# An earlier load gate, reordered matmuls and a different last product in a fused matmul, Gelu, matmul kernel

## Chip, cores and metric

One Trainium2 chip, one of its cores. The metric is the device time of one execution in microseconds. All runs quoted are of the fast state. The profile's span is about 1.75 us shorter than the measured time of the same execution (120.5 against 122.23 before, 119.0 against 120.74 after). Times inside an execution are counted from the span's start.

## The reference

```python
m, k, n, p = 1024, 1024, 2048, 1024          # a: m x k, b: k x n, c: n x p, all float32
h = np.matmul(a, b)
h = 0.5 * h * (1 + np.tanh(np.sqrt(2 / np.pi) * (h + 0.044715 * h ** 3)))
return np.matmul(h, c).astype(np.float32)
```

## The kernel before

Half of the first product (1024 of the 2048 columns of b) is computed directly, transposed (hT = b^T a^T), in bf16. The other half of it, and all of the second product, run as a seven-product scheme of the Strassen kind ("Seven"): sums of operands are made on VectorE, seven products of half the size on TensorE, and the results are added up. The two products of operands as they are (P1, P2) are bf16; the five with a sum in them are f32r, a float32 form that the traces call fp32r. A product's result is added up in a bank of PSUM, from which ScalarE or VectorE takes it.

Loads come on two queues. SP's queue brings the f32 data that must be there first: pieces of a (512 KB, `load_a(h, q)`), to be cast and transposed, and half-pieces of b (`load_b(q, c)`). GpSimd's queue casts to bf16 on the way: the other pieces of a, the slices k=4..7 of b, then the rest of b and c. A one-element copy, `gate`, holds this queue back until a given f32 load has landed.

```python
load_a(0, 0); load_b(0, 0); load_a(1, 0); load_a(0, 1)      # f32 loads one to four
load_b(1, 0); load_a(1, 1); load_b(0, 1); load_b(1, 1)      # five to eight

nc.gpsimd.tensor_copy(gate, sta[:, 1, 1, 3, 0:1])           # waits for load six
...                                                         # then GpSimd issues a, b[k=4..7], b2, c

block(0, range(4), (0, 1))              # bf16 matmuls of slices k=0, 1
turn1(1, 0, 5, cast_a(1, 0, nc.vector))  # cast, 8 transposes on TensorE, copy out
turn1(0, 1, 7, cast_a(0, 1, nc.scalar))
...
block(1, range(3), (0, 1))
cast_b(2, 0); cast_b(3, 0)              # ScalarE
ab = cast_a(1, 1, nc.vector)            # load six
block(0, range(4), (2,))
turn1(1, 1, 7, ab)
block(0, range(4), (3,))
for k in range(KH):                     # KH = 4, KT = 8
    cast_b(k, 1)                        # ScalarE: loads seven and eight
for t in range(4):
    leave(0, t)                         # empties PSUM banks, ScalarE for even t
...
for h, t in T2[:7]:                     # seven tiles, k=0..3 done before
    mm1(ps[h, t], t, h, range(KH, KT))  # k=4..7, tile by tile
    gelu(t, h, ps[h, t])
```

The second product, `two`, by stages (X are PSUM banks 0 to 3, Y banks 4 to 7):

```python
for j in range(4):                                   # P1: A11 B11, bf16
    w.product(px[j], A11, B11, j, True)
    p1[j] = snap("m", px[j], "p1")                   # ScalarE keeps a copy
for j in range(4):                                   # P2: A12 B21, bf16
    p = bank(Y[j])
    w.product(p, A12, B21, j, True)
    done(0, 0, j, plus(p, p1[j]))                    # VectorE add, store of C11
...                                                  # P5, P6, P7, P3: f32r
for j in range(4):                                   # P4, last: C21, VectorE copy, store
    w.product(px[j], w.s[3], w.last_t, j, False)
    done(1, 0, j, px[j])
```

## Time and profile before

| | before |
|---|---|
| time, median of 4 | 122.32 us (122.23 to 122.36) |
| profiled span | 120.5 us |
| TensorE (PE) busy | 112.4 us, 93% |
| VectorE (DVE) busy | 88.4 us, 73% |
| last matmul ends | 116.72 us |
| from there to the end of the span | 3.75 us |

TensorE is the bound, but a busy share of 93% does not say where the missing time is. Three questions do: where between two matmuls is there a hole (the timeline and the wait view of PE), what ended it, and what comes after the last matmul. The prediction shows these lines.

### The profile page before, as it was taken

To read this page: it belongs to the slowest core of one execution; us is meant where nothing else is said; L and a number is where in the kernel's file an instruction comes from. 1 tells how busy PE (TensorE), PEld (TensorE's weight loads), DVE (VectorE), ACT (ScalarE), POOL (GpSimd) and SP (SyncE) were. 2 spreads that over 40 slices of the span, in tenths; PEclk is the share of its full clock that TensorE was granted. 3 is DMA by queue.
4 is the path that set the end of the run, shared out by engine and by line. 5 is a ranking of instruction groups with operands and counts; after the bars stand their busy time and mean duration, and the time that the engine had idled before them with its cause. 6 is when DMAs were issued, how large, how long until landed. Compare 5 with 4: busy or idle time off the path is not lost.

```text
span 120.5 us, 1459 instructions
## 1 busy us (share of the span) xinstructions
PE 112.4 (93%) x550; PEld 72.7 (60%) x550; DVE 88.4 (73%) x92; ACT 53.3 (44%) x86; POOL 14.6 (12%) x27
## 2 busy tenths in 40 slices
PE   6985999969999999999999999999999999999970
PEld 2633545624444444888888444468888888888850
DVE  0243589488017899978779999979999996892490
ACT  4046490005637779946669636900012595100000
POOL 2000895462322000000000000000000000000000
PEclk9999999999999999999999999999999999999997
DMA  2999999999999999997000000062000002004695
GB/s 85 283 371 367 305 167 202 168 205 207 207 207 213 212 212 209 212 212 145 1 5 0 5 0 0 0 250 98 0 0 0 5 0 87 0 0 174 235 352 197
DMA packets 11463, 16.86 MB, mean 140 GB/s; under 512 B 705, under 2 KB 5825, under 8 KB 11457
## 3 DMA queue, kind: packets, MB, share of 16 engines
q0 software_dynamic: 5952, 8.39, 40.1%
q1 hardware_dynamic: 5504, 8.39, 19.8%
q8 instruction: 4, 0.07, 0.2%
q14 instruction: 3, 0.02, 0.1%
HBM read 20.97 MB, written 4.19 MB: 209 GB/s over the span
## 4 chain that ended last, share of the span: by engine, by line
PE 62%; DMA 21%; DVE 6%; POOL 4%; SPq 2%; issue 1%; ACT 1%; DVEq 0%; ACTq 0%
PE ps L239 50%; PE ps L112 12%; DMA b<-in_b_dram 8%; DMA sta<-in_a_dram 8%; DMA out_dram<-ot 5%; DVE x L197 4%; POOL a L93 2%; DVE ot L285 2%; POOL b L96 1%; SPq L68 1%; SPq L71 1%; DVE ot L370 1%; ACT u L280 1%; POOL gate L82 0%; DVEq L285 0%
## 5 line engine op out<-in xcount | busy, mean ns | idle before, releaser
L112 PE MATMUL ps<-aT,b 128*128 128x512 bf16 x128 | 29.2, 379 | 1.7 <-DMA b<-in_b_dram 1.2
L239 PE MATMUL ps<-x,s 128*128 128x512 f32 x128 | 29.6, 391 | 0.0
L239 PEld LDWEIGHTS ps<-x,s 128*128 128x128 f32 x128 | 24.0, 188 | 5.1
L112 PEld LDWEIGHTS <-b 128*128 128x128 bf16 x128 | 12.1, 98 | 15.9 <-DMA b<-in_b_dram 2.0
L239 PE MATMUL ps<-x,x 128*128 128x512 f32 x64 | 14.8, 389 | 0.0
L239 PE MATMUL ps<-c_sb,hT 128*128 128x512 bf16 x64 | 14.0, 379 | 0.0
L239 PEld LDWEIGHTS ps<-x,x 128*128 128x128 f32 x64 | 12.0, 188 | 2.5
L280 ACT ACTIVATE v<-ps 128x512 f32<-128x512 f32 x8 | 4.8, 599 | 17.1 <-PE ps L239 17.1
L116 ACT ACTIVATE hT<-ps 128x512 bf16<-128x512 f32 x12 | 6.8, 595 | 12.1 <-PE ps L112 12.1
L239 PE MATMUL ps<-x 128*128 128x512 f32 x48 | 11.3, 393 | 0.0
L239 PEld LDWEIGHTS <-hT 128*128 128x128 bf16 x64 | 6.2, 97 | 7.6 <-issue 0.3
L270 DVE TENSOR_TENSOR half<-ps,half 128x512 f32<-128x512 f32 x8 | 5.5, 692 | 7.0 <-PE ps L112 6.6
L239 PEld LDWEIGHTS ps<-x 128*128 128x128 f32 x48 | 9.0, 188 | 2.0
L197 DVE TENSOR_TENSOR x<-c_sb 128x1024 fp32r<-128x1024 bf16 x8 | 9.2, 1215 | 0.0
L285 DVE TENSOR_TENSOR ot<-ps,v 128x512 f32<-128x512 f32 x8 | 5.3, 687 | 4.6 <-DMA out_dram<-ot 3.8
L141 ACT ACTIVATE b<-stb 128x512 bf16<-128x512 f32 (+1 forms) x9 | 4.7, 573 | 6.6 <-DMA stb<-in_b_dram 6.6
L285 DVE TENSOR_TENSOR ot<-ps,u 128x512 f32<-128x512 f32 x8 | 5.4, 691 | 3.0 <-ACT u L280 3.0
L116 ACT ACTIVATE hT<-ot 128x512 bf16<-128x512 f32 x12 | 7.0, 624 | 1.2 <-DVE ot L285 1.2
L239 PE MATMUL ps<-aT,b 128*128 128x512 bf16 x32 | 7.1, 379 | 0.0
L102 POOL DMA_DIRECT2D c_sb<-in_c_dram x8 | 5.7, 712 | 8.9 <-DMA b<-in_b_dram 8.9
L280 ACT ACTIVATE p<-ps 128x512 f32<-128x512 f32 x8 | 4.6, 594 | 4.8 <-PE ps L239 4.8
L116 ACT ACTIVATE hT<-half 128x512 bf16<-128x512 f32 x8 | 5.0, 631 | 2.6 <-DVE half L270 2.6
(47 smaller groups left out, 114.7 us busy)
## 6 DMA issues: line engine op xcount, KB each, us to landing
c_sb<-in_c_dram POOLq DMA_DIRECT2D x8, 512.0 KB, 20.2
out_dram<-ot SPq DMA_DIRECT2D x16, 256.0 KB, 2.1
sta<-in_a_dram SPq DMA_DIRECT2D x4, 512.0 KB, 6.9
stb<-in_b_dram SPq DMA_DIRECT2D x4, 512.0 KB, 8.9
b<-in_b_dram POOLq DMA_DIRECT2D x4, 512.0 KB, 13.8
a<-in_a_dram POOLq DMA_DIRECT2D x4, 256.0 KB, 5.6
b<-in_b_dram POOLq DMA_DIRECT2D x4, 256.0 KB, 8.9
```

The source lines that it names most:

```text
L68: nc.sync.dma_start(out=sta[:, h, q], in_=av[:, 4 * h:4 * h + 4, ds(q * 256, 256)])
L71: nc.sync.dma_start(out=stb[:, c, 2 * q:2 * q + 2], in_=bv[:, 2 * q:2 * q + 2, ts(c, H)])
L93: nc.gpsimd.dma_start(out=st, in_=av[:, 4 * h + m:4 * h + m + 2, ds(KH * 128, H)])
L102: nc.gpsimd.dma_start(out=c_sb[:, t:t + 2], in_=cv[:, t:t + 2])
L112: nc.tensor.matmul(p, b1[:, k, ts(t, 128)], aT[:, h, k], start=(k == k0), stop=(k == k1 - 1))
L116: nc.scalar.activation(hT[h][:, t], p, AF.Gelu_apprx_tanh)
L141: nc.scalar.activation(b1[:, k, ds(c * H + i * (H // n), H // n)], stb[:, c, k, r], AF.Copy)
L197: nc.vector.tensor_tensor(out=dst[:, r], in0=x[:, r], in1=y[:, r], op=op)
L239: nc.tensor.matmul(p[:, ds(c0, w)], l[:, k, ts(j, 128)], r[:, k, ds(c0, w)], start=(start and k == 0), stop=(k == self.kt - 1), skip_group ...
L270: nc.vector.tensor_tensor(out=half[:, h, t], in0=p, in1=half[:, h, t], op=ADD)
L280: nc.scalar.activation(st, p, AF.Copy)
L285: nc.vector.tensor_tensor(out=ot, in0=p, in1=st, op=ADD)
```

## The change

It has four parts. The gate looks at load five instead of load six. Three matmuls are put in front of the transposes that waited for ScalarE. In the first product the slices k=4..7 go over four tiles slice by slice. And in the second product the C11 tile j=3 keeps its P1 in a buffer of its own in SBUF until the end, while its P2 product (eight matmuls of 512 columns) becomes the last work of the kernel, in two column halves of 256, each added and stored by itself.

The diff leaves out the hunks that only fold the function `last` into `done`.

```diff
-    nc.gpsimd.tensor_copy(gate, sta[:, 1, 1, 3, 0:1])
+    nc.gpsimd.tensor_copy(gate, stb[:, 0, 3, 0:1])
@@
-    turn1(0, 1, 7, cast_a(0, 1, nc.scalar))
     for t in range(3):
         ps[1, t] = bank(4 + t)
-    block(1, range(3), (0, 1))
+    ab = cast_a(0, 1, nc.scalar)
+    block(1, range(3), (0,))
+    turn1(0, 1, 7, ab)
+    block(1, range(3), (1,))
@@
-    for h, t in T2[:7]:
-        mm1(ps[h, t], t, h, range(KH, KT))
+    for k in range(KH, KT):
+        for h, t in T2[:4]:
+            mm1(ps[h, t], t, h, (k,))
+    for n, (h, t) in enumerate(T2[:7]):
+        if n >= 4:
+            mm1(ps[h, t], t, h, range(KH, KT))
         gelu(t, h, ps[h, t])
@@ (P1)
-            p1[j] = snap("m", px[j], "p1")
+            if w is two and j == 3:
+                p1[j] = pieces("ab", 2, [128, H], F32, "p1")
+                nc.scalar.activation(p1[j], px[j], AF.Copy)
+            else:
+                p1[j] = snap("m", px[j], "p1")
@@ (P2)
-        for j in range(4):
+        for j in range(4 if w is one else 3):
@@ (after P4)
+        if w is two:
+            for i in range(2):
+                r = ds(i * 256, 256)
+                p = bank(Y[i])
+                w.product(p, A12, B21, 3, True, i * 256, 256)
+                ot = pieces("e", 2, [128, 256], F32, "ot")
+                nc.vector.tensor_tensor(out=ot, in0=p[:, r], in1=p1[3][:, r], op=ADD)
+                store(3, i * 256, 256, ot)
```

More of the change, by code (lines that the diff above doesn't have):

```diff
@@ L323, in seven @@
             w.product(px[j], w.s[3], w.last_t, j, False)
-            if w is one or j < 3:
-                done(1, 0, j, px[j])
-            else:
-                last(px[j])
+            done(1, 0, j, px[j])
+        if w is two:
[6 more added lines that the diff above has]
+                store(3, i * 256, 256, ot)
     one.s1()
@@ L372, in done2 @@
         store(4 * i + j, l * H, H, p)
-    def last(p):
-        done2(1, 0, 3, p)
     def between2(n):
```

## The prediction

> **What bounds the kernel now.** I read the page first. Its chain of waits is almost all TensorE from 27 us on, and before that it is loads:
>
> ```profile
> span 120.5 us, 1459 instructions
> ...
> PE   6985999969999999999999999999999999999970
> ...
> PE ps L239 50%; PE ps L112 12%; DMA b<-in_b_dram 8%; DMA sta<-in_a_dram 8%; DMA out_dram<-ot 5%; DVE x L197 4%; POOL a L93 2%; DVE ot L285 2%; POOL b L96 1%; SPq L68 1%; SPq L71 1%; DVE ot L370 1%; ACT u L280 1%; POOL gate L82 0%; DVEq L285 0%
> ```
>
> The first line with PE is its busy tenths in 40 slices, the second the chain by line. The row of tenths shows where time is still to be had: slices 2 to 4 (3 to 12 us), the "6" of slice 9 (24 to 27 us), and the tail. Everything between 27.3 and 116.7 us is dense, so a change pays there only by taking out TensorE work. TensorE's waits and its timeline name the holes:
>
> ```profile
> PE pt L135 <- ACT ab L106: 1.3, 1, 1.3
> ...
> PE ps L112 <- DMA b<-in_b_dram: 1.2, 2, 0.8
> ...
> 10.93 0.62 PE L135 MATMUL pt<-ident,ab 128*128 128x128 bf16 x8 [1.31 <-ACT ab L106]
> ...
> 13.55 0.61 PE L135 MATMUL pt<-ident,ab 128*128 128x128 bf16 x8
> ...
> 24.30 1.46 PE L112 MATMUL ps<-aT,b 128*128 128x512 bf16 x6
> ...
> 26.09 0.39 PE L112 MATMUL ps<-aT,b 128*128 128x512 bf16 x1 [0.34 <-DMA b<-in_b_dram]
> 27.33 1.04 PE L112 MATMUL ps<-aT,b 128*128 128x512 bf16 x4 [0.85 <-DMA b<-in_b_dram]
> ```
>
> The first product has four banks ready at 25.2 us, but it goes tile by tile: after two matmuls of its first tile (k=4, 5) it waits for slice k=6 (26.09) and k=7 (27.33). Counted by starts at 0.216 us each, 26.09-25.59 plus 27.33-26.31 is 1.5 us lost (the wait view says 1.2, as it counts a matmul as busy until its modelled end).
>
> The loads before that run on two queues. The f32 queue (SP) brings eight 0.52 MB loads; the casting queue (POOL) starts when the gate copy sees load six:
>
> ```profile
> 11.13 1.15 ACT L141 ACTIVATE b<-stb 128x512 bf16<-128x512 f32 x2 [0.25 <-DMA stb<-in_b_dram]
> ...
> 12.64 0.18 POOL L82 COPY gate<-sta 128x1 f32<-128x1 f32 x1 [11.33 <-DMA sta<-in_a_dram]
> 12.68 0.69 DVE L108 CAST ab<-sta 128x1024 bf16<-128x1024 f32 x1 [0.40 <-DMA sta<-in_a_dram]
> ...
> 13.96 1.15 ACT L141 ACTIVATE b<-stb 128x512 bf16<-128x512 f32 x2 [1.68 <-DMA stb<-in_b_dram]
> ...
> 15.27 1.15 ACT L141 ACTIVATE b<-stb 128x512 bf16<-128x512 f32 x2 [0.15 <-DMA stb<-in_b_dram]
> ...
> 16.32 2.04 ACT L106 ACTIVATE half<-ps 128x512 f32<-128x512 f32 x4
> ```
>
> So loads 5, 6, 7 and 8 land at about 11.1, 12.6, 13.95 and 15.25. The tail:
>
> ```profile
> 109.30 7.42 PE L239 MATMUL ps<-x,s 128*128 128x512 f32 x32
> ...
> 114.62 2.03 DVE L370 COPY ot<-ps 128x512 f32<-128x512 f32 x3
> 116.83 0.69 DVE L370 COPY ot<-ps 128x512 f32<-128x512 f32 x1 [0.18 <-PE ps L239]
> ```
>
> The last matmul ends at 116.72; copy 0.69, store about 2.1 (the page's time to landing of a store), close 0.8 us. The chain in order of time also reaches 116.8 by a second way, vector add, store, vector add, each waiting for an output buffer; it ends in the same 0.1 us as TensorE, so both must move for the end to move.
>
> **What the Trainium skill says.** "TensorE: Matmul & The Clock Gate", "Wait — 56ns, not 53.3ns?": warm back-to-back matmuls start N/2.4 GHz plus about 2.5 ns apart, 215.7 ns at 512 columns and 55.6 at 128. The trace agrees: 59 matmuls in 12.90 us from 28.63, so (12.90-0.38)/58 = 0.216 us, and eight transposes in 0.61 give 0.056. By the same formula 256 columns cost 0.109 (an estimate; this trace has none). "DMA: Bandwidth & Descriptors", "Queues, rings and completion order": each engine takes turns between the queues it has work for, packet by packet. So a casting load started sooner takes bandwidth from the f32 loads still under way; before shows hardly any such overlap. Same page, "Anatomy of one DMA — SWDGE (gpsimd) path": a DMA has a fixed cost of about 2.0 us plus bytes over 436 GB/s. For stores here the trace has 2.1 us for 256 KB, so the fixed part must be smaller, about 1.4.
>
> **The change part by part.**
>
> 1. Slice by slice. Sixteen matmuls (k=4..7 on four banks) replace the tile-by-tile order. Slice k is first used at 25.16, 26.03, 26.89, 27.75; k=6 and k=7 were there at 26.05 and 27.3 even before. No wait is left: -1.5 us, with no matmul added. The Gelus come in a bunch of four (0.60 each), but banks 0 to 3 are wanted again only after 20 more matmuls (4.3 us), so they hide.
>
> 2. The first reordering. Three matmuls that wait only for the copy ending 10.35 go ahead of the transposes that waited for ScalarE until 10.93. TensorE fills 10.4 to 11.05, but the next thing, the transposes at 13.55, needs the VectorE cast 12.68+0.69 = 13.37 of load six, which nothing moves. So of 0.6 us filled only about 0.12 us survives (13.55 to 13.43).
>
> 3. The gate looks at load five, not six: casting starts 1.5 us sooner (11.13 for 12.64). Gain alone: with part 1, the b slices are no longer what TensorE waits for, so **nothing**. Cost: loads seven and eight now share the engines. Summing half-microsecond windows of DMA, 3.70 MB of the f32 queue's 4.19 have moved by 13.0 us; that is about when casting data should begin (gate 11.2 plus the 1.4 to 1.9 us seen between the gate at 12.64 and the drop of the rate at 14.0 to 14.5). The remaining 0.5 MB at half of 0.38 MB/us takes 2.6 us instead of 1.4, so load eight lands up to 1.2 us later (16.4); if casting ramps as slowly as before (100 to 160 GB/s written at 14.5 to 16.5), the delay is half that. I take d = 0.7. This matters because ScalarE casts loads seven and eight **before** it empties bank 0: copies at 15.27 (two), then the emptying 16.32 to 16.91, and TensorE wants bank 0 at 13.99 + 14 x 0.216 = 17.01. There is 0.1 us of slack in before and none after part 2. So d comes back almost whole as a TensorE wait.
>
> Front end together: -1.5 -0.12 +0.7 = **-0.9 us**, between -0.4 (d = 1.2) and -1.6 (d = 0).
>
> 4. The last work. Eight bf16 matmuls (8 x 0.216 = 1.73 us) leave the second product's P2 stage and come back at the end as sixteen of 256 columns (16 x 0.109 = 1.75): TensorE sum +0.02. What the stages between need must come 1.73 us sooner too. VectorE is nearly full there (20.8 of 22 us between 80 and 102), so this is the place to check: in before it idles 0.88 us at 79.65 waiting for the fourth P2 product and then adds for 0.69; both go, so its chain of sums starts 1.55 us sooner. The tightest use is the last quarter of T3 (ends 94.84, wanted at 94.75 + 6 x 0.23 = 96.1); it keeps 1.1 us of its 1.3. So TensorE stays dense. The vector-store chain hangs on the T4 sums and moves along. At the end a 256-wide add replaces the 512-wide copy: 512 columns took 0.69, of which 512/0.96 GHz = 0.53 streams (estimate; the clock from the Trainium skill's first page, "Trainium Kernel Development and Optimization", "NeuronCore Architecture"), leaving 0.16 fixed, so 256 cost about 0.42: -0.27. The last store has 128 KB for 256: at about 0.35 MB/us, -0.37. With the other half's store beside it I take -0.6 for both, together with +0.02 **-0.6 us**.
>
> Sum: 122.3 - 0.9 - 0.6 = **120.8 us**.
>
> **The rivals.** (a) The gate is free, d = 0: the f32 loads keep their rate through the slow ramp of casting. For it: at 14.0 to 14.5 casting had begun and load eight still landed with its usual 0.8 us behind its bytes. Against: only 0.1 MB was left then. Time: 120.1. (b) The gate costs d = 1.2 to 1.5, most of what the slices gain: "the wait removed comes back at bank 0". For it: equal turns, and no slack at 16.91. Time: 121.2 to 121.6. (c) VectorE becomes the bound in the second product because TensorE asks 1.7 us sooner: against it stand the 1.55 us that its own chain gains. If its order of buffers, now shifted by one, cost another store's wait (2.1 us), the tail's gain would be gone: 121.4 or more. (d) The reordering and the slices do nothing since the c loads bound later: against, the DMA rate falls to almost zero at 57 us while c is first summed at 64.
>
> **Range and chances.** Best case 1.6 + 0.65 = 2.25 us, or 1.8%: 2% (2.45 us) is beyond the sum of all I found, unless the early start moves load six's cast too. Worst case 0.3 in front and 0.3 at the end: 121.7. Eight in ten: 120.0 to 121.6. Within 2% 0.91, faster 0.08, slower 0.01.
>
> **What would show it.** Part 1: no wait for b near 26 us, and in the 24 to 27 us slice a 9 for the 6. Part 2: matmuls at 10.4, transposes still at about 13.4. Part 3: gate near 11.2; ScalarE's third pair of casts of the second half of b at 15.8 to 16.4 for 15.27; a TensorE wait on ScalarE's emptying of bank 0 near 17 us of about d. If there is none, rival (a). Part 4: sixteen matmuls in about 1.75+0.1 us, an add near 0.42, last matmul to end of span 3.2 us for 3.8; no TensorE wait between 65 us and the end. The prediction is wrong if load six itself lands later than 12.6, if VectorE waits longer for output buffers, or if the 256-column matmuls run above 0.12 us each.

## The result

The changed kernel took 120.66 us (median of 4, 120.54 to 120.74) against 122.32. A ratio here is the mean time of one kernel's fast runs over the mean of the other's of the same rounds, so not quite the ratio of the medians: 0.9865, 95% interval 0.9847 to 0.9882, or 1.65 us. The prediction said 120.8, so the sum was right. The profile shows that its parts were not.

The front of the changed kernel: TensorE's waits, then lines of the timeline (start, length, engine, instruction, idle time before it and what ended it).

```profile
PE ps L112 <- ACT b L141: 0.9, 1, 0.9
PE ps L112 <- DVE aT L136: 0.8, 1, 0.8
PE pt L135 <- DVE ab L108: 0.5, 1, 0.5
```

```profile
10.33 0.81 PE L112 MATMUL ps<-aT,b 128*128 128x512 bf16 x3 [0.78 <-DVE aT L136]
...
11.28 0.18 POOL L82 COPY gate<-stb 128x1 f32<-128x1 f32 x1 [9.97 <-DMA stb<-in_b_dram]
...
12.78 0.70 DVE L108 CAST ab<-sta 128x1024 bf16<-128x1024 f32 x1 [0.39 <-DMA sta<-in_a_dram]
...
13.54 0.62 PE L135 MATMUL pt<-ident,ab 128*128 128x128 bf16 x8
...
14.06 1.15 ACT L141 ACTIVATE b<-stb 128x512 bf16<-128x512 f32 x2 [1.67 <-DMA stb<-in_b_dram]
...
15.38 1.15 ACT L141 ACTIVATE b<-stb 128x512 bf16<-128x512 f32 x2 [0.17 <-DMA stb<-in_b_dram]
16.44 2.04 ACT L106 ACTIVATE half<-ps 128x512 f32<-128x512 f32 x4
...
24.30 5.99 PE L112 MATMUL ps<-aT,b 128*128 128x512 bf16 x26
```

No wait for a slice of b is left, and from 24.30 on the matmuls run through. The waits in the early part are still there under other names, and the transposes of load six start at 13.54 as they did at 13.55, though load six itself was cast 0.10 us later (12.78 for 12.68). The gate opens at 11.28, yet ScalarE gets loads seven and eight at 14.06 and 15.38, only 0.1 us later than before (13.96, 15.27). As load five was 0.11 us later too (cast from 11.24 for 11.13), the time from there to the cast of load eight is 4.14 us in both: the delay that the prediction feared is not there.

The tail of the changed kernel, from its timeline:

```profile
106.05 7.41 PE L241 MATMUL ps<-x,s 128*128 128x512 f32 x32
...
113.30 1.92 PE L241 MATMUL ps<-c_sb,hT 128*128 128x256 bf16 x16
113.64 0.69 DVE L386 COPY ot<-ps 128x512 f32<-128x512 f32 x1 [0.22 <-DMA out_dram<-ot]
114.39 0.42 DVE L342 TENSOR_TENSOR ot<-ps,p 128x256 f32<-128x256 f32 x1
115.26 0.42 DVE L342 TENSOR_TENSOR ot<-ps,p 128x256 f32<-128x256 f32 x1 [0.45 <-PE ps L241]
```

The add takes 0.42 us for the copy's 0.69, as worked out. But TensorE ends at 115.22 and the span at 118.97: 3.75 us, exactly as before. All of the 1.5 us by which the span is shorter (120.47 to 118.97) is there when the last matmul ends (116.72 to 115.22). The new tail brought nothing. Two misses, a front that gained more and a tail that gained less, cancelled in the sum by luck.

The place to look is what SP does after the last store. The page counts no semaphore instruction as busy, so its views show these only as SP's own waits. This is SP's wait view, first of before, then of after:

```profile
SPq L419 <- DMA out_dram<-ot: 1.2, 2, 0.7
```

```profile
SPq L432 <- DMA out_dram<-ot: 1.5, 1, 1.5
```

Before waits for the landing of stores twice, after once and longer. The records of SP's instructions in the trace, which the views leave out, give the rest (start in us of the last store, of the closing waits on semaphores, and of the drain after them):

```
        last store  closing waits                                                        drain
before  117.55      117.93 118.00 118.06 118.13 118.19 118.25 118.31 118.82 [119.59]      119.65
after   115.72      116.09 [117.67] 117.73 117.79 117.85 117.91 117.98 118.03 118.10      118.16
```

The bracket marks the wait that the last landing ends (landings at 119.57 and 117.65). SP goes through its waits in a fixed order, one every 0.061 us. There are eight semaphores, used in turn by its eight f32 loads and then by its stores; the first wait of each row is for none of them. Before makes 16 stores, so the last is on the eighth semaphore and its wait is the last one. After makes 17, so the last is on the first semaphore again, and seven more waits follow its landing: 118.16-117.67 is 0.49 us for 0.07, or 0.43 us given back. That is a theory from two traces; it is tested below.

### The profile page after: what moved, and what is told of

Its sections match the earlier page's. It is cut to its first block, busy times and chain, and to the rows that moved or that the text cites. A ratio compares the mean times of both kernels' runs of the same rounds, so it can differ in the third digit from the quotient of the medians.

```text
span 119.0 us, 1467 instructions
## 1 busy us (share of the span) xinstructions
PE 111.3 (94%) x552; PEld 72.6 (61%) x558; DVE 88.5 (74%) x93; ACT 52.7 (44%) x86; POOL 14.6 (12%) x27
## 4 chain that ended last, share of the span: by engine, by line
PE 85%; DMA 8%; SPq 2%; DVE 1%; issue 1%; DVEq 0%
PE ps L241 63%; PE ps L112 20%; DMA sta<-in_a_dram 8%; PE pt L187 2%; SPq L68 1%; SPq L71 1%; DVE ab L108 1%; PE pt L135 1%; DVE ot L342 0%; DVEq L108 0%
## 5 line engine op out<-in xcount | busy, mean ns | idle before, releaser
L241 PE MATMUL ps<-c_sb,hT 128*128 128x512 bf16 (+1 forms) x70 | 14.1, 355 | 0.1
L241 PEld LDWEIGHTS <-hT 128*128 128x128 bf16 x72 | 6.9, 98 | 7.1 <-issue 0.5
L116 ACT ACTIVATE hT<-ps 128x512 bf16<-128x512 f32 x12 | 6.3, 603 | 11.0 <-PE ps L112 11.0
L108 DVE CAST ab<-sta 128x1024 bf16<-128x1024 f32 x3 | 2.1, 694 | 5.3 <-DMA sta<-in_a_dram 5.3
```

The lines of the kernel that those rows point to most:

```text
L108: nc.vector.tensor_copy(dst, src)
L116: nc.scalar.activation(hT[h][:, t], p, AF.Gelu_apprx_tanh)
L241: nc.tensor.matmul(p[:, ds(c0, w)], l[:, k, ts(j, 128)], r[:, k, ds(c0, w)], start=(start and k == 0), stop=(k == self.kt - 1), skip_group ...
```

## The experiments

Theories before the first run. **A**: the slices alone make the front's gain, the gate only makes the same slices come sooner, so the two buy the same microseconds. **B** (rival): the gate makes it. **C** (rival, the prediction's own): casting loads started sooner take turns with the f32 loads and delay them. **D**: the new tail gains 0.4 us and the order of SP's closing waits gives it back. **E** (rival): the tail gains or loses by chance. All eleven kernels gave correct results, in the fast state.

| run | what | ratio to before, 95% interval |
|---|---|---|
| e1_slices | before + slices | 0.9866 (0.9844 to 0.9889) |
| e2_gate | before + gate at load five | 0.9886 (0.9861 to 0.9911) |
| e3_tail | before + new last work | 0.9996 (0.9986 to 1.0006) |
| e4_reorder | before + reordering | 1.0005 (0.9990 to 1.0020) |
| e5_after_24stores | after, 24 stores | 0.9813 (0.9787 to 0.9839) |
| e6_before_17stores | before, 17 stores | 1.0024 (1.0015 to 1.0032) |
| e7_gate3 | after, gate at load three | 0.9966 (0.9953 to 0.9979) |
| e8_act_extra | after + one ScalarE cast | 0.9909 (0.9895 to 0.9922) |
| e9_gate1 | after, gate at load one | 1.0421 (1.0401 to 1.0441) |
| e10_tail_24stores | before + new last work, 24 stores | 0.9953 (0.9936 to 0.9970) |
| e11_slices_tail_24stores | before + slices + new last work, 24 stores | 0.9843 (0.9809 to 0.9878) |

### e1_slices: the slices alone

The edit is the third hunk of the diff, put into before.

> Before plus the slice order alone. Theory A (the slices were already in time, only their order of use was wrong): TensorE's waits for b at 26 us vanish and it gains 1.5 us, ratio about 0.988; no more than 0.1 us is left for the earlier gate. Rival B (the earlier gate made the gain): k=7 lands at 27.3 as before, and with less work ahead TensorE still waits; gain under 0.7 us.

120.79 us, ratio 0.9866: the whole gain of the change (0.9865). Theory A holds, B falls. The timeline of TensorE in this kernel:

```profile
23.96 0.61 PE L185 MATMUL pt<-ident,a 128*128 128x128 bf16 x8
24.40 3.83 PE L112 MATMUL ps<-aT,b 128*128 128x512 bf16 x17
```

The gate was at load six here, and ScalarE's last pair of casts of b still began at 15.37, as in the changed kernel (15.38). In e8 below, with the gate at load five, it was 15.25. The 0.1 us between before and after at this place is within what executions differ by, whatever the gate.

### e2_gate: the gate alone

The edit is the first hunk, put into before.

> Before plus the earlier gate alone, tiles still one by one. Theory A: b lands 1.1 us sooner as in the changed kernel (k=7 at about 26.2), so the wait shrinks from 1.5 to about 0.4 us: gain 1.1, ratio about 0.991. The gate and the slices then buy the same microseconds, and their gains don't add. The f32 loads seven and eight land at most 0.15 us later, with no wait of TensorE near 17 us. Rival B: gain as large as of the whole change, 1.6. Rival C (equal turns on the DMA engines): load eight is 0.7 us or more late and the gain is under 0.5.

121.08 us, 0.9886: 1.4 us gained. In GpSimd's timeline, the issues of c that wait for slices of b come at 23.83, 25.15 and 26.39 in place of 25.01, 26.34 and 27.57: b lands 1.2 us sooner. Of the two holes of before, start to start at 26.09 and 27.33, one is left: 0.31 us lost before the matmul that starts at 26.14. So gate and slices cover the same hole, and having both (0.9865) is worth no more than the slices alone. The two intervals overlap; that the gate alone is 0.2 us the weaker one rests on the trace's 0.31 us. Theory A's forecast of 1.1 us (0.991) is just inside the interval, B's 1.6 too; e1 decides between them. C's delay is not there: load eight is cast 4.15 us after load five, as before (4.14).

### e3_tail and e10_tail_24stores: the new last work, with 17 and with 24 stores

e3 is the P1, P2 and P4 hunks put into before. e10 is e3 with the three stores of C11 made in P2, at about 78 us where the queue is quiet, cut into ten pieces:

```diff
-        store(4 * i + j, l * H, H, p)
+        if (i, l) == (0, 0):
+            n = (4, 3, 3)[j]
+            cut = [32 * (16 * c // n) for c in range(n + 1)]
+            for c in range(n):
+                store(j, cut[c], cut[c + 1] - cut[c], p[:, cut[c]:cut[c + 1]])
+        else:
+            store(4 * i + j, l * H, H, p)
```

That makes seven stores more, none of them near the end: 24 in all, so the last is on the eighth semaphore.

> Before plus the new last work alone. Theory D: the last landing comes 0.4 us sooner after TensorE's end, but SP waits for the last store's semaphore as second of its eight closing waits, not as the last, and the six or seven waits after it cost 0.06 us each: 0.4 us are given back, time as before within 0.15 us. Rival E (the closing differs between runs by chance, the tail does gain): 0.4 us or more faster, ratio 0.997 or less.

> Before plus the new last work, with 24 stores so that the last lands on the last semaphore. The new last work alone was worth nothing (0.9996). Theory D: its own gain of 0.4 us shows once the seven closing waits are gone: ratio 0.9965, within 0.0015. Rival: the gain is not there even so, ratio 0.9985 or more.

e3 is worth nothing (0.9996). e10, the same tail with more stores, is 0.9953, or 0.57 us faster than before. This is the wait view of SP in e10; it waits twice again, as before did:

```profile
SPq L432 <- DMA out_dram<-ot: 1.0, 2, 0.6
```

### e5_after_24stores and e6_before_17stores: the closing alone

e5 is the changed kernel with the edit of e10. e6 is before with one early store cut in two, nothing else:

```diff
+        if (i, l, j) == (0, 0, 0):
+            store(0, 0, 256, p[:, 0:256])
+            store(0, 256, 256, p[:, 256:512])
+        else:
+            store(4 * i + j, l * H, H, p)
-        store(4 * i + j, l * H, H, p)
```

> The changed kernel with its first three stores of C11, in a quiet stretch at 77 us, cut into ten pieces, so that 24 stores are made and the last one lands on the last of the eight semaphores. Theory D: SP's closing waits after the last landing shrink from seven to one or none: 0.4 us faster than the changed kernel, about 120.2 us, ratio to before about 0.983. Rival E: as the changed kernel, 0.9865, within 0.001.

> Before with nothing changed but its first store of C11 at 78 us cut in two, so that 17 stores are made and the last one is on the first of the eight semaphores. Theory D (closing waits in a fixed order): the last landing comes when it did, and seven waits of 0.06 us follow it: 0.4 us slower than before, ratio 1.0035. Rival E: the number of stores is nothing to the closing, ratio 1.000.

e5 is 0.9813 (120.09 us) against the changed kernel's 0.9865, about 0.6 us faster; e6 is 1.0024, 0.3 us slower than before: less than the 0.4 expected (1.0035 lies just outside its interval), but clear of zero, and the trace shows the whole 0.42 (0.89 against 1.31 in the table). In both directions, by a store that lies 40 us before the end, the end of the kernel moves. SP's wait view in e6, one long wait as in the changed kernel where before has two:

```profile
SPq L423 <- DMA out_dram<-ot: 1.6, 1, 1.6
```

Theory D holds. The profiled executions, in us:

| | before | after | e3 | e10 | e11 | e6 |
|---|---|---|---|---|---|---|
| stores | 16 | 17 | 17 | 24 | 24 | 17 |
| last matmul's end to last store's issue | 0.84 | 0.49 | 0.49 | 0.49 | 0.49 | 0.93 |
| issue to last landing | 2.02 | 1.94 | 1.93 | 1.85 | 1.85 | 2.03 |
| last landing to end of span | 0.89 | 1.32 | 1.31 | 0.88 | 0.89 | 1.31 |
| sum | 3.75 | 3.75 | 3.74 | 3.22 | 3.23 | 4.27 |

e5's trace has 3.23 too (its f32 loads ran late in the execution that was profiled, so its span of 119.1 us is not that of its median). Add for copy brings 0.35 us, of which 0.27 is the shorter instruction; the rest is that the add starts 0.04 us after the last matmul, while before's copy started 0.12 after it, by the chain view after an earlier store had landed (116.71) and freed its output buffer. The half-sized store brings only 0.1 to 0.2, and the closing costs 0.43 whenever the number of stores leaves the last one on the first semaphore. With 24 stores the tail is 3.22 us, the figure that the prediction gave.

### e4_reorder: three matmuls in the first hole

The edit is the second hunk, put into before.

> Before plus the reordering around the transposes of the second piece of a alone. Theory: three matmuls move into the hole at 10.4 us, but the transposes of load six still start at 13.5, bound by VectorE's cast of load six; time as before within 0.15 us, ratio 1.000. Rival: the 0.6 us filled at 10.4 survive, ratio 0.995.

1.0005: nothing. TensorE's timeline in e4 shows why:

```profile
10.35 0.81 PE L112 MATMUL ps<-aT,b 128*128 128x512 bf16 x3 [0.78 <-DVE aT L136]
10.99 0.61 PE L135 MATMUL pt<-ident,ab 128*128 128x128 bf16 x8
11.65 1.75 PE L112 MATMUL ps<-aT,b 128*128 128x512 bf16 x6
13.35 0.62 PE L135 MATMUL pt<-ident,ab 128*128 128x128 bf16 x8
```

The hole at 10.4 is filled, and TensorE stands still before 13.35 instead, until VectorE has cast load six. The time alone would not show a small gain, though: before's holes at 26 us, which end when slices of b land, are still in this kernel. TensorE comes to them sooner (its matmuls there start at 24.11 for 24.30) and waits longer, until the same moment as before (26.09, 27.33):

```profile
26.10 0.39 PE L112 MATMUL ps<-aT,b 128*128 128x512 bf16 x1 [0.53 <-DMA b<-in_b_dram]
27.34 1.04 PE L112 MATMUL ps<-aT,b 128*128 128x512 bf16 x4 [0.85 <-DMA b<-in_b_dram]
```

What the reordering does at its own place is read from the start of load six's cast to the transposes: 0.75 us in e4 (12.60 to 13.35), 0.76 in the changed kernel (12.78 to 13.54), against 0.87 in before, e1 and e2. So 0.11 us survives there, as the prediction had it, and not the 0.6 of the rival.

### e8_act_extra: does a delay at ScalarE come back at bank 0?

The changed kernel with a repeat of the last cast in front of the emptying of bank 0:

```diff
     for k in range(KH):
         cast_b(k, 1)
+    cast_b(3, 1)
```

> The changed kernel with one more ScalarE cast of 128x512 (a repeat of the last one, 0.58 us in the group's mean, 0.53 from start to start) in front of the emptying of bank 0. The prediction's step that a delay d at ScalarE comes back whole at bank 0: emptying ends near 17.5 us, TensorE wants the bank at 17.0; it waits 0.45 to 0.55 us and the whole is that much slower than the changed kernel, ratio to before about 0.9905. Rival: there is more slack, or the hole is given back later by another wait: ratio as the changed kernel's 0.9865 within 0.001.

121.25 us, 0.9909: 0.5 us slower than the changed kernel, for a delay of 0.53. ScalarE's and TensorE's timelines in e8:

```profile
15.25 1.81 ACT L141 ACTIVATE b<-stb 128x512 bf16<-128x512 f32 x3 [0.17 <-DMA stb<-in_b_dram]
16.97 2.04 ACT L106 ACTIVATE half<-ps 128x512 f32<-128x512 f32 x4
...
17.60 2.75 PE L112 MATMUL ps<-aT,b 128*128 128x512 bf16 x12 [0.48 <-ACT half L106]
```

So the prediction's step from d to a wait at bank 0 was right. What it had wrong was d.

### e7_gate3 and e9_gate1: when do the two queues really share?

The changed kernel with the gate at load three, and at load one:

```diff
-    nc.gpsimd.tensor_copy(gate, stb[:, 0, 3, 0:1])
+    nc.gpsimd.tensor_copy(gate, sta[:, 1, 0, 3, 0:1])      # e7
+    nc.gpsimd.tensor_copy(gate, sta[:, 0, 0, 3, 0:1])      # e9
```

> The changed kernel with the gate two loads sooner still, at load three (seen at about 8.2 us, for 11.2). Theory F (a late start of the casting queue is what kept d small: its packets came only at 13.9 us, when 0.1 MB of f32 was left): with casting packets from 10 to 11 us on the two queues take turns, loads six to eight land 0.7 us or more late, ScalarE empties bank 0 later than 17.0 and TensorE waits; 0.5 to 1.5 us slower than the changed kernel. Rival G (casting packets wait until the f32 queue is nearly drained, wherever the gate is): first casting packet still near 13.9, time as the changed kernel, ratio 0.9865 within 0.0015.

e7 is 121.99 us, 0.9966: 1.2 us slower than the changed kernel. Its timeline, GpSimd, ScalarE and TensorE:

```profile
8.12 0.70 POOL L82 COPY gate<-sta 128x1 f32<-128x1 f32 x1 [6.81 <-DMA sta<-in_a_dram]
8.76 2.99 POOL L93 DMA_DIRECT2D a<-in_a_dram  x4
...
16.63 1.15 ACT L141 ACTIVATE b<-stb 128x512 bf16<-128x512 f32 x2 [1.48 <-DMA stb<-in_b_dram]
17.68 2.04 ACT L106 ACTIVATE half<-ps 128x512 f32<-128x512 f32 x4
...
18.31 1.89 PE L112 MATMUL ps<-aT,b 128*128 128x512 bf16 x8 [1.16 <-ACT half L106]
```

Load eight is cast 1.25 us later (16.63 for 15.38), and TensorE waits for bank 0. From the packet records of the trace: between 13.5 and 14.5 us 97 casting and 94 f32 packets were started, so here, with both queues at work, they take equal turns (in e9 130 and 130 in the same microsecond). That is theory C (F in the text on record), with d = 1.25 where the prediction gave up to 1.2 for half a megabyte shared; here 0.40 MB was. But rival G had half of it: although the gate opened 3.2 us sooner than in the changed kernel, the first casting packet came only 0.8 us sooner.

> The changed kernel with the gate at load one (seen at about 4.4 us). With the gate at load three the first casting packet came at 13.15 us, five us after the gate, with 0.40 MB of f32 left. Theory H (the casting queue gets its first turn only when little more than the last f32 load is left, however soon it is issued): first packet again at 13.0 to 13.3, load eight cast at about 16.6, time as with the gate at load three, ratio 0.997 within 0.002. Rival: the lag grows with the queue but does not stop there; first packet before 12.5, more than 0.6 MB of f32 shared, load eight after 17.5 and time as before or slower, ratio over 1.002.

e9 is 127.60 us, 1.0421. Theory H falls: the first casting packet came at 9.10 us, with 1.89 MB of f32 data still to move. Load six is cast at 15.97 for 12.78, load eight at 22.08 for 15.38. TensorE's longest wait in e9, and the clock row of its page:

```profile
PE pt L135 <- DVE ab L108: 3.2, 1, 3.2
```

```profile
PEclk9999955999999999999999999999999999999998
```

From within that wait on, 15.62 to 22.44 us, TensorE was also granted half its clock (eleven matmuls at 0.427 us start to start instead of 0.216, 17.98 to 22.24; the two fives in the row), so not all of the 6.9 us over the changed kernel are waits. The start of casting in six executions, from the trace's DMA records:

| | before | after | e2 | e5 | e7 | e9 |
|---|---|---|---|---|---|---|
| gate copy starts | 12.64 | 11.28 | 11.20 | 11.88 | 8.12 | 4.13 |
| first issue on GpSimd | 12.76 | 11.39 | 11.31 | 12.00 | 8.76 | 4.77 |
| f32 data not landed at that issue, MB | 0.62 | 1.11 | 1.14 | 0.89 | 2.08 | 3.37 |
| first casting packet | 14.43 | 13.91 | 14.05 | 13.76 | 13.15 | 9.10 |
| issue to first packet | 1.67 | 2.52 | 2.74 | 1.76 | 4.39 | 4.33 |
| f32 data moved from then on, MB | 0.02 | 0.13 | 0.07 | 0.18 | 0.40 | 1.89 |

With more f32 data still to come the casting queue waited longer for its first turn, up to 4.4 us; from 2.08 to 3.37 MB the wait grew no more. The number of loads alone does not set it: e5 and the changed kernel both have their gate at load five, and waited 1.76 and 2.52 us. What holds the queue back is open: these runs do not tell a backlog of f32 work that the engines had already taken up from a slower start at GpSimd.

### e11_slices_tail_24stores: without the gate and the reordering

Before with the slices, the new last work and the edit of e10.

> Before plus the slices and the new last work with 24 stores; gate at load six and transposes as before. If the earlier gate and the reordering are worth nothing beside the slices: 120.2 us, ratio 0.983, as the changed kernel with 24 stores (0.9813). If they carry something: 0.2 us or more slower than that.

120.29 us, 0.9843. Beside e5 (0.9813) that is 0.2 us slower by the medians and 0.37 by the ratios, by the letter of the expectation the side of "they carry something"; but the intervals overlap, one of e11's six runs took 121.50, and e1 against the changed kernel (0.9866, 0.9865) shows no difference. In the profiled executions, counted from the start of load six's cast, the last matmul ends 102.44 (changed kernel) and 102.46 us (e5) later with gate and reordering, 102.50 (e1) and 102.65 (e11) without. So no run shows clear of noise that the gate or the reordering carries anything beside the slices; 0.1 to 0.2 us, and by the intervals a little more, could be there. Both e5 and e11 have lower medians than before and after.

## Why the prediction was right, and where not

Its total was right (120.8 for 120.66, range 120.0 to 121.6). Its parts were -0.9 us in front and -0.6 at the end; the runs show about -1.6 and 0.

- **Part 1, "-1.5 us, with no matmul added"**: right. e1 alone measures 0.9866, 1.6 us, and no wait is left.
- **Part 2, "only about 0.12 us survives"**: right at its place, for the reason given, the cast of load six: 0.11 us from that cast to the transposes (e4 and the changed kernel). Whether it reaches the end is not shown: in e4 the holes at 26 us would swallow it (0 within 0.2 us), and beside the slices it is lost in the noise.
- **Part 3, gain "nothing" beside part 1**: right, e1 and the changed kernel have the same ratio. Alone the gate gains 1.4 us (e2), of the same hole.
- **Part 3, cost "I take d = 0.7"**: wrong, and the main miss in front. The step that failed is "that is about when casting data should begin", 13.0 us, which took the lag of 1.4 to 1.9 us from before, where only two f32 loads had yet to land when the gate opened. In the changed kernel the lag was 2.5 us (first issue to first packet), casting began at 13.91, 0.13 MB was shared and not 0.5, and d was 0.0 counted from load five. That goes beyond the late start: by equal turns 0.13 MB at half of 0.38 MB/us would still cost 0.3 us (an estimate), and why it cost nothing is open. The rest of the chain is what e7 and e8 show: equal turns with a d of 1.25 once 0.40 MB was shared, and bank 0 without slack. So rival (a) is what happened; rival (b) happens when the gate is two loads sooner.
- **Part 4, TensorE and VectorE**: right. The sums kept up, no wait of TensorE after 65 us; the add took 0.42. That it also starts 0.08 us sooner after the last matmul was not in the sum.
- **Part 4, "At about 0.35 MB/us, -0.37" for the store**: wrong term. Halving the store saved 0.09 us (2.02 to 1.94), up to 0.17 in e10. The prediction had put the fixed part of a store at 1.4 us; by these two sizes it is 1.7 to 1.85 (an estimate: 2.02 less twice the saving).
- **Part 4, the close**: taken as 0.8 us, the same for both kernels; none of the rivals said that the number of stores could matter. It cost 0.43 us (e3 against e10, e6 against before) and made the tail's 0.4 us vanish. With the store's term that is the 0.6 us of the tail; d was too large by about as much, 0.7, and so the sum came out right: luck, not understanding.
- **Its signs of being wrong**: two showed faintly. Load six was cast at 12.78 for 12.68, but load five was late by as much. VectorE's waits for output buffers grew from 3.8 to 4.0 us, by the 0.22 before its copy at 113.64; TensorE did not wait for it.

## What to carry to other kernels

Two edits that close the same hole do not add; put each into the old kernel alone before crediting either. And a hole that ends at a fixed landing swallows any small gain made before it, so a null result of the time needs a look at the trace. When a change adds or removes a load or store of that queue, look at the order in which the kernel's end waits for the stores: the last one should be on the semaphore that is waited for last (only stores were added here). A lag measured beside a nearly drained queue says little about the same lag beside a full one (1.67 us against 4.4 here), so an estimate that rests on it wants a range as wide as the queue's backlog.

## What the Trainium skill lacked or had wrong

- No page has it: SP's closing waits went through the semaphores of its stores in a fixed order, 0.061 us each, so a last landing on the first of eight cost 0.43 us more than one on the last (e6, e3 and e10).
- "DMA: Bandwidth & Descriptors", "Queues, rings and completion order": turns by packet agree with e7 (97 to 94 packets in one microsecond), but the page gives no lag of a second queue's first turn behind a first queue's backlog: 1.67 us from first issue to first packet with two f32 loads yet to land (before), 1.8 to 2.7 with three (e5, after, e2), 4.3 to 4.4 with five or seven (e7, e9). Its figure of about 1 us to the first byte for this path ("Specifications") does not hold behind such a backlog; no run here has the casting queue alone.
- The same page, "Anatomy of one DMA — SWDGE (gpsimd) path": 2.0 us plus bytes over 436 GB/s, stated for the other queue (the prediction set it beside SP's stores all the same), would be 2.60 us for a store of 256 KB and 2.30 for one of 128 KB (estimates), 0.30 apart. SP's last store took 2.02 and 1.94 (1.85 in e10), so the formula is too long for SP's stores; the fixed part that they show, 1.7 to 1.85 us, lies between its 2.0 and the 1.4 that the prediction preferred.
